# Where side work is issued in a Mamba-2 scan: one step per piece of the scan instead of one behind the projection, and later exponentials in three groups

## The chip, the cores and the metric

The kernel runs on one core of a Trainium2 chip, as one program from input to output. The metric is the time of one execution on the device in microseconds (us). TensorE (PE) multiplies matrices, with its weight loads shown apart (PEld); VectorE (DVE) does elementwise work on tensors; ScalarE (ACT) does activations, casts and copies; GpSimd (POOL) and SyncE (SP) here mostly issue transfers. ACT and POOL issue transfers too. The granted clock is the share of TensorE's full speed that the throttle allowed in a stretch of time.

## The reference

One layer of a trunk over 528 positions (16 meta tokens and 512 tokens) with 1024 channels:

```
u = rmsnorm(h, mix_norm_w)
proj = u @ w_in                       # pool, z, x, B, C, dt, two gates
y_pool = pool_mixer(u_pool, ...) @ w_pool_up
xbc = silu(causal_depthwise_conv(xbc, conv_w, conv_b))     # width 4
y = ssd_chunked(xs, dt, -exp(a_log), B, C) + xs * d_skip   # 8 groups of 4 heads of 64, state 128, chunks of 128
y = rmsnorm per group (y * silu(z)) * norm_w
h = h + (gate_pool * y_pool + gate_ssd * (y @ w_ssd_out)) @ w_o
v = rmsnorm(h, mlp_norm_w)
out = rmsnorm(h + relu(v @ w_ff1)**2 @ w_ff2, final_norm_w)[:, 16:]
```

In one chunk of ssd_chunked, with a_cs the running sum of dt*a:

```
y_diag = (C B^T * exp(a_cs[l] - a_cs[s]) masked) @ (x * dt)
y_off  = (C @ state before the chunk) * exp(a_cs[l])
state  = exp(a_cs[last]) * state + B^T @ (exp(a_cs[last] - a_cs) * x * dt)
```

## The kernel before, in words

**Precision and weights.** All is float32. A product is made of three matmuls of halves: an operand is split into a high part (ACT casts it, L94, `whi`) and a low part (DVE subtracts, L96, `wlo`), and TensorE multiplies high by high, high by low (L196) and low by high (L198). Weights come in blocks of 128 x 1024 from SP's queue into `raw`, three buffers deep, four deep for `whi` and `wlo`.

**Fewer multiplications.** Some products are made with the seven multiplications of Strassen and Winograd on halves. They need sums of weights and sums of u. A set of *weight sums* (`weight_steps`) is formed in DRAM by transfers on POOL's queue alone (L747 and L753): first copies, then transfers that add, in four rounds for a set of kind fx or f1 and two for f2; each round waits for the one before. *Sums of u* (`sums_of_u`) take, for k = 0 to 3, two tiles of u from DRAM (L869, POOL's queue, tiles `ra` and `rb` of one buffer each), combine them on DVE (`combine`, L874 to L877) and split the two results (`form`, L882 on ACT, L883 on DVE, into `t0h`, `t0l`, `t1h`, `t1l`), after which `ra` and `rb` are free for the next k. In the groups of X_PAIRS (4 to 7) the x part of the projection is made that way (`pair`, tiles `rawp`, loaded at L466, split into `whip`, `wlop`); the weight sums of the sets fx feed it.

**The scan.** Behind the norm and the first projections the program goes through eight groups of heads, g = 0 to 7. `ssd(g)` is the scan of group g, cut by its yields into pieces:

- piece 1: the running sums `abc` of group g are loaded (POOL's queue); B and x are transposed on TensorE (`ptb`, `ptm` at L590, `ptx` at L598); DVE makes `xdt` and `xdd`; ACT makes `eb`, the two exponentials of L610 at which y_off is scaled, the differences of decays (L615, L622 with DVE) and their exponentials (`decay`).
- piece 2: C times B (`pcb`), the states `st` (L650) and the masked decays (L653 on DVE, in place in `abc`).
- pieces 3 and 4: for either half of the group's y, TensorE's `po` (L662, from the states) and `py` (L668, from the masked decays), and DVE's L671 to L675 (`yt`).
- then the norm of the group: squares, sums over partitions (`png`), reciprocals (L691, `rs`), and the split into `yh` and `yl`, which ssd's output product reads.

`group_proj(g + 1)` projects the next group meanwhile: B and C, then x (convolution of four taps, L420 and before, then silu, L422, tile `xc`), a gate in groups 1 to 3, then z with its silu (L563 for both halves at once). In group 4 also `out_half` (half of the output product) and in group 7 `out_part` (L848, `psp`) are among the fill. `weave(a, b, n)` sets the order in which the program is written: one piece of the scan, then one step of the first list in `b` that is not at its end (n steps with n = 2), and again. The lists in `b` are used up one after another:

```
fill = [group_proj(g + 1, ...)]          # or out_part; in group 4 out_half ahead of it
fill.append(sums_of_u(SUMS_AT[g], g))    # g = 0: k = 0; g = 1: k = 1; g = 2: k = 2 and 3
fill.append(weight_sums_at())            # SETS_AT[g] times
```

so sums of u come behind all of the projection, and weight sums last. The engines run their queues in order. Where an instruction is to come behind another in its queue though the data does not ask for it, `tc.issue_after` says so: `combine` behind the masked decays (L653) or the squares, `form` behind the first state or the squares, the exponentials `eb` behind the last silu of x of the same group (`x_ready`), which lies in the projection that goes beside the scan of the group before, and the weight sums' transfers behind a one-column copy on POOL (`seen`) of `mark`, which is a tile that the scan wrote last, so that a round does not start ahead of the scan's piece.

Of the kernel before, what the change touches and what calls it, by code (L numbers as in the profile page):

```python
# [11 lines left out]
AF = mybir.ActivationFunctionType  # L12
# [35 lines left out]
SUMS_AT = {0: (0,), 1: (1,), 2: (2, 3)}  # L48
# [2 lines left out]
BC_PAIRS = ()  # L51
PAIRS = [(k, g) for g in range(G) for k in "bx" if g in (BC_PAIRS if k == "b" else X_PAIRS)]

SETS_AT = {0: 1, 1: 1, 2: 1, 3: 1, 4: 2, 5: 1, 6: 1}
SETS_POOL = 2

PLAIN = 4
# [6 lines left out]
def kernel(ctx: ExitStack, tc, xT, x, w, fx, f1, f2, vec, fnw, out):  # L64
# [344 lines left out]


    mark, first_part = [None], [True]
    x_ready, filled = {}, {}

    def conv(dst, src, ct):
        n = dst.shape[-1]
# [92 lines left out]
    def group_proj(g, cur, gate=None):  # L508

        first = g == 0  # L510
        xc, bt, ct, zt = cur

        def plain(dst, t, skip):
            if first and (dst is bt or dst is ct):
                view = viewB if dst is bt else viewC
            else:
                runs, view = wide(psum2(f"px{g}_{t}"), skip)
                proj(runs, block(), X if first else U)
            conv(dst, first_raw(t, view, skip) if first else view, t)

        def z_half(ps, i):

            with tc.issue_after(done[0].ins) if g == 1 else nullcontext():
                wt = block()
            proj(narrow(ps), wt, X if first else U)

        bcs = ((bt, 16 + g, 0), (ct, 24 + g, NM - 4))
        xs = ((xc[:, 0, :], 2 * g, 0), (xc[:, 1, :], 2 * g + 1, 0))
        both = g in BC_PAIRS
        for kind, ts, paired in (("b", bcs, both), ("x", xs, g in X_PAIRS)):  # L530
            if paired:
                r = raw_pair(kind, g)
                yield from pair(kind, g, r)
                for (dst, t, skip), src in zip(ts, r):
                    conv(dst, src[:, skip:], t)
                yield
            else:
                for t in ts:
                    plain(*t)
                    filled.setdefault(g - 1, mm[0])  # L540
                    yield
            if both:
                i = 0 if kind == "b" else 1
                ps = psum2(f"pz{g}_{i}")[:, :SEQ]
                z_half(ps, i)
                act.activation(zt[:, i, :], ps, AF.Silu)
                yield
        if both:
            return
        if gate is not None:  # L550
            gate_pool(gate)
            yield
        ps = psum2(f"pz{g}")
        for i in range(2):
            z_half(ps[:, i * SEQ : (i + 1) * SEQ], i)
        zf = zt.rearrange("p i t -> p (i t)")
        if first:
            dve.tensor_tensor(zt, ps.rearrange("p (i t) -> p i t", i=2),
                              rsb[:, NM:].unsqueeze(1).to_broadcast([P, 2, SEQ]), op=ALU.mult)
            act.activation(zf, zf, AF.Silu)  # L560
            mark[0] = zf[:, :1]
        else:
            act.activation(zf, ps, AF.Silu)  # L563
        yield


# [3 lines left out]
    def ssd(g, cur):  # L570
# [35 lines left out]
        ap = abc.rearrange("p (i j) l -> p i j l", j=2)  # L606
        for j in range(2):
            js = slice(64 * j, 64 * j + 64)
            with tc.issue_after(x_ready[g].ins):
                act.activation(eb[js, :, :], ap[js, :, j, :], AF.Exp)  # L610
        dm = abc.rearrange("p r (c l) -> p r c l", c=4)
        for r in range(R):
# [89 lines left out]

    done, abc_load, masked, y_first, squared, b_meta, x_decayed = {}, {}, {}, {}, {}, {}, {}

    def weave(a, b, n):

        end = object()
        a = [a]
        while a or b:
            for s in [a] + [b] * n:  # L710
                if s and next(s[0], end) is end:
                    s.pop(0)

    m1 = {}

# [22 lines left out]
    def weight_steps():  # L738
        t = sets.pop(0)
        src = {"fx": fx, "f1": f1, "f2": f2}[t[0]][t[1]]  # L740
        o = {n: wsum[(*t, n)] for n in SUMS[t[0]]}
        put = nc.gpsimd.dma_start
        put(o["t1"], src[B11])
        end = put(o["s3"], src[B12])
        if "t2" in o:
            put(o["t2"], src[B22])
            end = put(o["t4"], src[B21])  # L747
        yield end
        put(o["t1"], src[B12], accum_op=ALU.add)
        yield put(o["s3"], src[B22], accum_op=ALU.add)  # L750
        if "t2" in o:
            yield put(o["t2"], o["t1"], accum_op=ALU.add)
            yield put(o["t4"], o["t2"], accum_op=ALU.add)  # L753
# [3 lines left out]
            pass  # L757
        return end

    def weight_sums_at():  # L760
        for _ in range(len(SUMS[sets[0][0]])):
            if not steps:
                steps.append(weight_steps())
            at = pool.tensor_copy(seen, mark[0])
            with tc.issue_after(at.ins):
                next(steps[0])
            yield
        assert next(steps.pop(), None) is None

    steps = []  # L770

    cur = group_tiles(0)
    early = weight_sums_at()
# [87 lines left out]
    def sums_of_u(ks, g):  # L861

        one, two = HF

        def load(k):
            a, b = raw_pair("u", k)
            with tc.issue_after(abc_load[g].ins):
                for t, kk in ((a, k), (b, k + 4)):
                    nc.gpsimd.dma_start(t, u_d[kk])  # L869
            return a, b  # L870

        def combine(a, b, behind):
            with tc.issue_after(behind[g].ins):
                dve.tensor_tensor(b[:, two], a[:, two], b[:, two], op=ALU.subtract)  # L874
                dve.tensor_tensor(a[:, two], a[:, one], a[:, two], op=ALU.subtract)
                dve.tensor_tensor(a[:, one], b[:, two], a[:, one], op=ALU.subtract)
                dve.tensor_tensor(b[:, one], b[:, one], a[:, one], op=ALU.add)  # L877

        def form(k, n, src, behind):
            hi, lo = T[n, "h", k], T[n, "l", k]  # L880
            with tc.issue_after(behind[g].ins):
                act.copy(hi, src)  # L882
            dve.tensor_tensor(lo, src, hi.bitcast(F32), op=ALU.subtract)  # L883

        t = load(ks[0])
        yield
        combine(*t, masked)
        yield
        form(ks[0], "0", t[0], y_first)
        yield  # L890
        form(ks[0], "1", t[1], y_first if len(ks) > 1 else squared)
        if len(ks) > 1:
            t = load(ks[1])
        yield
        if len(ks) > 1:
            yield
            combine(*t, squared)
            form(ks[1], "0", t[0], squared)
            yield
            form(ks[1], "1", t[1], squared)  # L900
            yield

    for g in range(G):
        nxt = group_tiles(g + 1) if g + 1 < G else None
        fill = [group_proj(g + 1, nxt, GATE_AT.get(g))] if nxt else [out_part()]
        if g == 4:
            fill = [out_half()] + fill
        if g in SUMS_AT:
            fill.append(sums_of_u(SUMS_AT[g], g))
        for _ in range(SETS_AT.get(g, 0)):  # L910
            fill.append(weight_sums_at())
        weave(ssd(g, cur), fill, 2 if g == 4 else 1)
        cur = nxt
    gc_stack.close()
    st_stack.close()
# [904 lines left out]
```

## Time and profile before

| | |
|---|---|
| time, median of 3 runs | 1026.56 us (1025.18 to 1030.13) |
| profiled execution | 1029.08 us, span 1027.4 us |
| mean granted clock | 0.992 |
| PE, PEld busy | 1001.4 us (97%), 881.5 us (86%) |
| DVE, ACT, POOL busy | 798.1 (78%), 611.9 (60%), 111.8 us (11%) |
| transfers | 184.51 MB, mean 180 GB/s |
| chain that ended last | PE 80%, DMA 6%, DVE 5%, ACT 5%, issue 3% |
| the scan of groups 0 to 7 | about 71 to 480 us of the span (first ptm to last py, L590 and L668) |

The profile is one execution; its times are microseconds from the start of its span. Busy counts an engine's instructions without the issue of transfers. PE and PEld overlap. A timeline row is start, duration, engine, line, operation, result <- operands, shapes, count, and in brackets the idle time just before it on that engine and what ended it. A row of a stretch is start:end, length, busy time (and instructions) of PE, PEld, DVE, ACT and POOL, the granted clock, the mean busy share of the 16 DMA engines, and GB/s.

### The profile page before, as it was taken

The page shows a single profiled execution, that of the slowest core. Times are in us where ns is not written, and L with a number is a line of the kernel's source. Part 1 is how long each engine was busy: PE and PEld are TensorE (multiplying, and loading weights), DVE is VectorE, ACT ScalarE, POOL GpSimd, SP SyncE. Part 2 cuts the span into 40 slices and gives each one's busy share as a digit, 9 for nine tenths or more (in the row PEclk, how much of TensorE's full clock was granted, in tenths as well). Part 3 has the DMA queues.
Part 4 walks back from the last instruction along what each step waited for, and adds up shares of the span by engine and source line. Part 5 has one row for each costly group of instructions (what it writes and reads, how often), then busy time and mean ns, then how long its engine had stood idle before and what let it go on. Part 6 is the DMA issues. An engine that isn't in the chain of part 4 may idle for free.

```text
span 1027.4 us, 15622 instructions
## 1 busy us (share of the span) xinstructions
PE 1001.4 (97%) x6047; PEld 881.5 (86%) x6047; DVE 798.1 (78%) x1153; ACT 611.9 (60%) x860; POOL 111.8 (11%) x183
## 2 busy tenths in 40 slices
PE   9998999998999979999999999999999999999997
PEld 7888998988888878987988888887889999999986
DVE  7976897967753668888589755876988888888885
ACT  7666859574934475775434433457756665665654
POOL 0420201010202201011330000231000000000000
PEclk9999999998999989999999999999999999999999
DMA  7593866444868937275895642789454554455432
GB/s 255 171 304 109 241 171 174 143 136 139 231 189 248 294 69 233 64 226 148 241 280 143 217 174 80 257 213 314 102 174 149 158 173 153 154 172 157 143 103 82
DMA packets 61291, 184.51 MB, mean 180 GB/s; under 512 B 7073, under 2 KB 8417, under 8 KB 60193
## 3 DMA queue, kind: packets, MB, share of 16 engines
q1 hardware_dynamic: 39456, 109.00, 32.5%
q0 software_dynamic: 18880, 69.67, 26.4%
q10 hardware_dynamic: 2880, 4.84, 1.3%
q8 instruction: 47, 0.77, 0.3%
q14 instruction: 28, 0.22, 0.1%
HBM read 173.13 MB, written 58.59 MB: 226 GB/s over the span
## 4 chain that ended last, share of the span: by engine, by line
PE 80%; DMA 6%; DVE 5%; ACT 5%; issue 3%; POOL 1%; SPq 0%; ACTq 0%; DVEq 0%; POOLq 0%
PE px L1439 8%; PE alpha L1507 6%; PE px L196 6%; PE px L1442 4%; PE px L198 3%; PE alpha L1510 3%; PE pz L196 3%; PE pgs L196 3%; PE pqx L485 2%; PE po L662 2%; DMA rawp<-in_fx 2%; PE py L668 1%; PE pso L128 1%; PE pz L198 1%; PE pso L129 1%
## 5 line engine op out<-in xcount | busy, mean ns | idle before, releaser
L94 ACT CAST whi<-raw 128x1024 fp32r<-128x1024 f32 (+2 forms) x90 | 90.0, 1012 | 87.5 <-DMA raw<-in_w 23.1
L96 DVE TENSOR_TENSOR wlo<-raw,whi 128x1024 fp32r<-128x1024 f32 (+2 forms) x90 | 105.0, 1172 | 40.1 <-ACT whi L94 31.0
L196 PE MATMUL px<-uh,whi 128*128 128x264 f32 (+1 forms) x320 | 83.3, 297 | 0.0
L198 PE MATMUL px<-ul,whi 128*128 128x264 f32 (+1 forms) x320 | 81.1, 290 | 0.0
L1214 DVE TENSOR_TENSOR ht<-ht,alpha 128x1024 f32<-128x1024 f32 x35 | 42.7, 1219 | 29.1 <-PE alpha L1507 29.1
L196 PEld LDWEIGHTS px<-uh,whi 128*128 128x128 f32 x320 | 62.2, 194 | 1.0 <-issue 0.7
L198 PEld LDWEIGHTS px<-ul,whi 128*128 128x128 f32 x320 | 61.9, 194 | 0.5 <-issue 0.2
L1137 ACT CAST shi<-rawf 128x1024 fp32r<-128x1024 f32 x42 | 44.2, 1052 | 28.7 <-PE alpha L1510 18.3
L1507 PE MATMUL alpha<-shi,hh 128*128 128x512 f32 x140 | 55.2, 394 | 0.0
L1510 PE MATMUL alpha<-shi,hl 128*128 128x512 f32 x140 | 54.7, 391 | 0.0
L1138 DVE TENSOR_TENSOR slo<-rawf,shi 128x1024 fp32r<-128x1024 f32 x42 | 51.2, 1219 | 0.6 <-ACT shi L1137 0.6
L1442 PE MATMUL px<-vsl,shi 128*128 128x256 f32 x192 | 47.4, 280 | 0.0
L1439 PE MATMUL px<-vsh,shi 128*128 128x256 f32 x192 | 47.4, 281 | 0.0
L196 PE MATMUL pz<-uh,whi 128*128 128x512 f32 x112 | 43.9, 392 | 1.3 <-ACT yh L698 1.3
L198 PE MATMUL pz<-ul,whi 128*128 128x512 f32 x112 | 43.8, 391 | 0.0
L196 PE MATMUL px<-uh,wlo 128*128 128x264 f32 (+1 forms) x320 | 42.3, 285 | 0.0
L196 PEld LDWEIGHTS px<-uh,wlo 128*128 128x128 f32 x320 | 40.5, 191 | 0.0
L1507 PE MATMUL alpha<-slo,hh 128*128 128x512 f32 x140 | 37.4, 389 | 0.0
L1439 PEld LDWEIGHTS px<-vsh,shi 128*128 128x128 f32 x192 | 36.2, 189 | 0.9
L1442 PEld LDWEIGHTS px<-vsl,shi 128*128 128x128 f32 x192 | 36.1, 188 | 0.9
L1442 PE MATMUL px<-vl,shi 128*128 128x256 f32 x144 | 36.1, 283 | 0.0
L1439 PE MATMUL px<-vh,shi 128*128 128x256 f32 x144 | 36.0, 282 | 0.0
(597 smaller groups left out, 3070.0 us busy)
## 6 DMA issues: line engine op xcount, KB each, us to landing
raw<-in_w SPq DMA_DIRECT2D x96, 512.0 KB, 4.6
f_t<-in_f POOLq DMA_DIRECT2D x38, 512.0 KB, 7.7
f_s<-in_f POOLq DMA_DIRECT2D x26, 512.0 KB, 8.1
b<-in_f SPq DMA_DIRECT2D x21, 512.0 KB, 4.6
rawf<-in_f SPq DMA_DIRECT2D x36, 256.0 KB, 3.0
rawf<-f_t SPq DMA_DIRECT2D x36, 256.0 KB, 2.9
abc<-acs_d POOLq DMA_DIRECT2D x8, 1024.0 KB, 6.0
f_t<-f_t POOLq DMA_DIRECT2D x12, 512.0 KB, 6.8
```

The costliest lines, as they stand in the source:

```text
L94: act.copy(hi[:, c], raw[:, c])
L96: dve.tensor_tensor(lo[:, c], raw[:, c], hi[:, c].bitcast(F32), op=ALU.subtract)
L196: pe.matmul(o, wt, rhs[0][k][:, c], start=part == 0 and k == 0, stop=part == 1 and k == NK - 1)
L198: mm[0] = pe.matmul(o, wt, rhs[1][k][:, c], start=False, stop=False)
L485: pe.matmul(o, wk, f[k][0], start=start and not low and k == 0, stop=stop and low == 1 and k == 3, skip_group_check=True)
L1137: splits.append((act.copy(hi, src), dve.tensor_tensor(lo, src, hi.bitcast(F32), op=ALU.subtract)))
L1138: dve.tensor_tensor(lo, src, hi.bitcast(F32), op=ALU.subtract)))
L1214: added[0] = dve.tensor_tensor(o, o, src, op=op)
L1439: pe.matmul(ps, m, f[k][0], start=start and not low and k == 0, stop=stop and low == 1 and k == 3, skip_group_check=True)
L1442: pe.matmul(ps, m, f[k][1], start=False, stop=False, skip_group_check=True)
L1507: pe.matmul(ps[t], hh[:, p, seg, st], m, start=bool(first and not low and p == 0), stop=bool(last and low and p == 1), skip_group_check=True)
L1510: pe.matmul(ps[t], hl[:, p, seg, st], m, start=False, stop=False, skip_group_check=True)
```

## The change

It has two parts.

*Order of the sums.* `weave` gets a fourth argument, `side`, a list of generators of which each takes one step in every round, behind the piece of the scan and the step of the fill. `sums_of_u` and `weight_sums_at` go into `side` instead of behind the projection in `fill`. `weight_sums_at(n)` runs n whole sets in a row with steps of its own, and ends with one more copy of `mark` for each set. The yields of `sums_of_u` are set anew: with two ks the second form of the first k and the load of the next one come in the same step, and the second form of the last k comes one step later. `SETS_AT` gives group 1 two sets and group 4 one (before, one and two).

*Exponentials.* `z_ready[g]` holds z's last silu of group g's projection. In groups 5 to 7 the two exponentials `eb` are issued behind it, and no longer behind `x_ready[g]`, the last silu of x.

```diff
--- before.py
+++ after.py
@@ -51,7 +51,7 @@
 BC_PAIRS = ()
 PAIRS = [(k, g) for g in range(G) for k in "bx" if g in (BC_PAIRS if k == "b" else X_PAIRS)]
 
-SETS_AT = {0: 1, 1: 1, 2: 1, 3: 1, 4: 2, 5: 1, 6: 1}
+SETS_AT = {0: 1, 1: 2, 2: 1, 3: 1, 4: 1, 5: 1, 6: 1}
 SETS_POOL = 2
 
 PLAIN = 4
@@ -409,7 +409,7 @@
 
 
     mark, first_part = [None], [True]
-    x_ready, filled = {}, {}
+    x_ready, z_ready, filled = {}, {}, {}
 
     def conv(dst, src, ct):
         n = dst.shape[-1]
@@ -543,7 +543,7 @@
                 i = 0 if kind == "b" else 1
                 ps = psum2(f"pz{g}_{i}")[:, :SEQ]
                 z_half(ps, i)
-                act.activation(zt[:, i, :], ps, AF.Silu)
+                z_ready[g] = act.activation(zt[:, i, :], ps, AF.Silu)
                 yield
         if both:
             return
@@ -557,10 +557,10 @@
         if first:
             dve.tensor_tensor(zt, ps.rearrange("p (i t) -> p i t", i=2),
                               rsb[:, NM:].unsqueeze(1).to_broadcast([P, 2, SEQ]), op=ALU.mult)
-            act.activation(zf, zf, AF.Silu)
+            z_ready[g] = act.activation(zf, zf, AF.Silu)
             mark[0] = zf[:, :1]
         else:
-            act.activation(zf, ps, AF.Silu)
+            z_ready[g] = act.activation(zf, ps, AF.Silu)
         yield
 
 
@@ -606,7 +606,7 @@
         ap = abc.rearrange("p (i j) l -> p i j l", j=2)
         for j in range(2):
             js = slice(64 * j, 64 * j + 64)
-            with tc.issue_after(x_ready[g].ins):
+            with tc.issue_after((z_ready if g in X_PAIRS[1:] else x_ready)[g].ins):
                 act.activation(eb[js, :, :], ap[js, :, j, :], AF.Exp)
         dm = abc.rearrange("p r (c l) -> p r c l", c=4)
         for r in range(R):
@@ -702,14 +702,15 @@
 
     done, abc_load, masked, y_first, squared, b_meta, x_decayed = {}, {}, {}, {}, {}, {}, {}
 
-    def weave(a, b, n):
+    def weave(a, b, n, side):
 
         end = object()
         a = [a]
-        while a or b:
+        while a or b or side:
             for s in [a] + [b] * n:
                 if s and next(s[0], end) is end:
                     s.pop(0)
+            side = [s for s in side if next(s, end) is not end]
 
     m1 = {}
 
@@ -757,17 +758,15 @@
             pass
         return end
 
-    def weight_sums_at():
-        for _ in range(len(SUMS[sets[0][0]])):
-            if not steps:
-                steps.append(weight_steps())
-            at = pool.tensor_copy(seen, mark[0])
-            with tc.issue_after(at.ins):
-                next(steps[0])
-            yield
-        assert next(steps.pop(), None) is None
-
-    steps = []
+    def weight_sums_at(n=1):
+        for _ in range(n):
+            steps = weight_steps()
+            while True:
+                at = pool.tensor_copy(seen, mark[0])
+                with tc.issue_after(at.ins):
+                    if next(steps, None) is None:
+                        break
+                yield
 
     cur = group_tiles(0)
     early = weight_sums_at()
@@ -887,29 +886,27 @@
         combine(*t, masked)
         yield
         form(ks[0], "0", t[0], y_first)
-        yield
-        form(ks[0], "1", t[1], y_first if len(ks) > 1 else squared)
         if len(ks) > 1:
+            form(ks[0], "1", t[1], y_first)
             t = load(ks[1])
         yield
+        yield
         if len(ks) > 1:
-            yield
             combine(*t, squared)
             form(ks[1], "0", t[0], squared)
             yield
-            form(ks[1], "1", t[1], squared)
-            yield
+        form(ks[-1], "1", t[1], squared)
+        yield
 
     for g in range(G):
         nxt = group_tiles(g + 1) if g + 1 < G else None
         fill = [group_proj(g + 1, nxt, GATE_AT.get(g))] if nxt else [out_part()]
         if g == 4:
             fill = [out_half()] + fill
+        side = [weight_sums_at(SETS_AT.get(g, 0))]
         if g in SUMS_AT:
-            fill.append(sums_of_u(SUMS_AT[g], g))
-        for _ in range(SETS_AT.get(g, 0)):
-            fill.append(weight_sums_at())
-        weave(ssd(g, cur), fill, 2 if g == 4 else 1)
+            side.append(sums_of_u(SUMS_AT[g], g))
+        weave(ssd(g, cur), fill, 2 if g == 4 else 1, side)
         cur = nxt
     gc_stack.close()
     st_stack.close()
```

## The prediction

> **What bounds the kernel now.** I read the page's engine table first, then who waited for whom, then the busy times by stretch, and last the timelines around the stretches in which TensorE stood still.
>
> ```profile
> PE 1001.4 (97%) x6047; PEld 881.5 (86%) x6047; DVE 798.1 (78%) x1153; ACT 611.9 (60%) x860; POOL 111.8 (11%) x183
> PE ptm L590 <- ACT xc L422: 5.7, 1, 5.7
> PE po L662 <- DVE st L650: 3.5, 3, 1.7
> 225.00:250.00 25.00, 20.84 (x147) 18.59 (x146) 19.80 (x36) 15.44 (x25) 0.56 (x1) 0.86 0.18 54
> 235.00:240.00 5.00, 2.38 (x21) 1.75 (x19) 5.00 (x9) 3.25 (x5) 0.00 (x0) 0.86 0.00 0
> 240.00:245.00 5.00, 5.00 (x23) 4.51 (x22) 2.50 (x5) 0.64 (x2) 0.00 (x0) 0.50 0.70 210
> 360.00:375.00 15.00, 9.34 (x52) 8.97 (x51) 8.44 (x17) 12.54 (x19) 0.81 (x1) 0.78 0.51 107
> 370.00:375.00 5.00, 5.00 (x25) 5.00 (x24) 3.42 (x8) 4.95 (x12) 0.00 (x0) 0.50 0.00 0
> ```
>
> The first line is the engines' busy time: TensorE is busy for 1001.4 of the span's 1027.4 us, so 26.0 us is all the idle time there is, and work taken from another engine is worth only what it takes out of that, or out of a lowered clock. The next two are the longest waits of TensorE. The rest are stretches: start and end, length, busy time of PE, PEld, DVE, ACT, POOL, then the granted clock, DMA share and GB/s. Two stretches of the scan hold most of what can be won there. At the start of group 3's scan TensorE is idle for 25.00 - 20.84 = 4.16 us, and over 240 to 245 it runs at 0.50. At the start of group 5's it is idle for 15.00 - 9.34 = 5.66 us and then runs at 0.50 over 370 to 375. Half a clock for 5 us is 2.5 us of work lost; with 0.86 of the 2.38 busy us before it, 0.3 more. So group 3's stop costs 4.16 + 2.5 + 0.3 = 7.0 us and group 5's 5.66 + 2.5 = 8.2 us: 15.2 together.
>
> The clock is where a rule speaks against my sum. In 225 to 250 no single wait is over 1.7 us (second row of waits), and the clock fell to 0.50 all the same. The Trainium skill, TensorE: Matmul & The Clock Gate, Part 1, says that the clock is halved after an idle window of about 3.4 us. By that, group 3's short waits would cost no clock and only 4.16 us could be won there, 2.8 us less; this trace has the halved clock after short waits, and the sum goes by the trace.
>
> **Why they stop: group 3.**
>
> ```profile
> 205.34 0.57 POOL L869 DMA_DIRECT2D rau<-u_d  x1 [1.73 <-DVE t0l L883]
> 208.00 0.86 POOL L869 DMA_DIRECT2D rbu<-u_d  x1
> 215.96 0.43 DVE L874 TENSOR_TENSOR rbu<-rau,rbu 128x264 f32<-128x264 f32 x1 [8.49 <-DMA rbu<-u_d]
> 217.72 3.38 DVE L691 RECIPROCAL rs<-rs 128x128 f32<-128x128 f32 x4
> 232.60 2.29 DVE L653 TENSOR_TENSOR abc<-abc,cbm 128x2048 f32<-128x2048 f32 x1 [1.49 <-ACT abc L622]
> DMA to landing us min/median/max: 3.4/8.0/11.6
> ```
>
> These are timelines (start, length, engine, line) and the landing times of the transfers of u_d. The fourth k of the sums of u is loaded at 205 to 208, because its two tiles have one buffer each and the third k was read out of them only then. DVE reached its combination (L874) with nothing landed and stood 8.49 us with everything of group 3 queued behind: the reciprocals of rs2, and through them ACT's decays, and L653, at which TensorE's py waits.
>
> **The change there.** In the changed program sums_of_u is a side list that takes one step per piece of the scan, no longer one after the whole of group_proj. On DVE the four instructions of k=2 now stand between the state updates of group 2 and its y, so that both tiles are free earlier.
>
> ```profile
> 186.53 0.41 DVE L650 TENSOR_TENSOR st<-st,pst 128x256 f32<-128x256 f32 x1
> 188.58 0.69 DVE L671 TENSOR_TENSOR yt<-po,eb 128x512 f32<-128x512 f32 x1 [0.97 <-PE po L662]
> 198.61 0.68 DVE L675 TENSOR_TENSOR yt<-yt,zt 128x512 f32<-128x512 f32 x1
> 199.21 0.42 DVE L875 TENSOR_TENSOR rau<-rau 128x264 f32<-128x264 f32 x1
> 204.34 0.70 DVE L883 TENSOR_TENSOR t0l<-rau,t0h 128x528 fp32r<-128x528 f32 x1
> ```
>
> The last readers (t0l, t1l, L883, 0.70 each) come just behind the first y product (188.58 + 0.69 = 189.3), so rau is free at about 190 and rbu at 191.3, 15 to 16 us before the 205.34 and 208.00 of now. With the median landing of 8.0 us rbu is there at 199.3. DVE's order has its combination behind the second half of y, which now ends at 199.3 (L675 at 198.6), and the two weight splits that moved out (2.4 us) about pay for the four combining steps and two L883 that moved in (1.7 + 1.4). So the wait of 8.49 becomes 0 to 2 us, and at the maximum landing of 11.6, 4 us. What is late next: raw blocks are prefetched three deep, and the split of the block before (wlo29) now stands behind that combination, so the cast of block 32 slips to about 208 on ACT, with xc3's silu, gp5, rs2 and the decays behind it. Counted on from there by the rows of now the decays end at about 226 to 228 instead of 232.57, and TensorE, without its gaps, comes to the py of group 3 at 233.5, after L653's 2.29 and the state updates. I take 6.5 of the 7.0 us as won; bounds 3 (landing at the maximum) and 7.0.
>
> ```profile
> 71.13 0.56 POOL L869 DMA_DIRECT2D rau<-u_d  x1 [4.88 <-PE pgp L196]
> 94.90 0.41 DVE L650 TENSOR_TENSOR st<-st,pst 128x256 f32<-128x256 f32 x1
> 85.00:95.00 10.00, 6.77 (x50) 6.16 (x49) 7.97 (x13) 7.42 (x10) 0.00 (x0) 0.84 0.00 1
> ```
>
> The other three combinations also move forward on DVE. For k=0 the loads go out behind the first four copies of set fx1, which wait for xdt0, at about 78.5 instead of 71.1; DVE comes to it after the last state update of group 0, near 95.3, so there are 16 us for them, and over 85 to 95 the DMA engines are idle. For k=1 and k=2 the loads have 10 us and more. Cost 0, and the cover is that margin.
>
> **Group 5.**
>
> ```profile
> 343.88 0.82 POOL L747 DMA_DIRECT2D f_t<-in_f  x1
> 365.25 0.81 POOL L753 DMA_DIRECT2D f_t<-f_t  x1 [8.28 <-DMA f_t<-f_t]
> 355.00:360.00 5.00, 5.00 (x24) 4.14 (x23) 1.90 (x2) 0.31 (x2) 0.81 (x1) 1.00 1.07 304
> 348.43 1.02 SPq L466 DMA_DIRECT2D rawp<-in_fx  x2
> 353.42 0.80 SPq L466 DMA_DIRECT2D rawp<-fx_t  x2
> DMA to landing us min/median/max: 2.5/4.6/11.5
> 360.43 1.05 ACT L94 CAST whip<-rawp 128x1024 fp32r<-128x1024 f32 x1 [5.12 <-DMA rawp<-in_fx]
> 364.13 0.64 ACT L422 ACTIVATE xc<-xc 128x528 f32<-128x528 f32 x1 [1.92 <-DVE xc L420]
> 364.79 1.28 ACT L610 ACT_TABLE_LOAD   x1
> 366.09 1.06 ACT L610 ACTIVATE eb<-abc 64x1024 f32<-64x1024 f32 x1
> 367.16 1.28 ACT L422 ACT_TABLE_LOAD   x1
> 368.45 0.64 ACT L422 ACTIVATE xc<-xc 128x528 f32<-128x528 f32 x1
> 369.15 0.69 PE L590 MATMUL ptm<-ident,xc 128*128 128x128 f32 x2 [5.66 <-ACT xc L422]
> ```
>
> Here two things stand in a row. Two sets of weight sums (SETS_AT 4: 2) run on POOL's queue from 320 to 373 behind group 4's out_half, the DMA share is 1.07, and the first pair of group 6's weights, issued at 348.43, lands so late that ACT stands 5.12 us at its cast (the longest landing of rawp is 11.5, the median 4.6). Then, between the two silus of xc5, ACT takes a table for exp, the first exponential eb and a table back: 1.28 + 1.06 + 1.28 = 3.62 us, while ptm waits for the second silu.
>
> The change takes both away. Set f12 is spread over group 4's own pieces (its copies behind xdt4, its sums behind st3_4 and yt4), one set moves to group 1, and the stretch 325 to 360 keeps only weight loads. With 4.6 us the pair of 348.43 lands at 353.0 and the next one, issued at 353.42, at 358.0. The exponentials come behind z's silu. On the other side the cast of that next pair (1.05) now stands between the two silus. Counted by the rows: the cast of 360.43 moves up by its wait of 5.12 to about 355.3, DVE's steps of xc5 end near 360.0 instead of 365.6, the first silu stands near 359, the cast behind it, and the second silu ends at 360.8. TensorE comes to ptm, now directly behind pz5, at 360.9. A stop of 0 to 1.5 us is left; I take 7.2 of the 8.2 us as won, bounds 0 (both pairs land as late as now: 353.42 + 11.5 + 1.05 + 0.64 = 366.6, which is 5.7 us of idle TensorE and the half clock again) and 8.2.
>
> **Groups 6 and 7 pay a little.**
>
> ```profile
> 422.96 1.04 ACT L622 ACTIVATE abc<-abc 128x1024 f32<-128x1024 f32 x1
> 424.04 2.29 DVE L653 TENSOR_TENSOR abc<-abc,cbm 128x2048 f32<-128x2048 f32 x1 [0.62 <-ACT abc L622]
> 427.66 1.09 PE L668 MATMUL py<-abc,xdt 128*64 128x128 f32 x14
> 465.81 0.74 PE L848 MATMUL psp<-yh,whi 128*128 128x512 f32 x2 [0.68 <-ACT whi L816]
> ```
>
> There was no stop at ptm to win in them. Both exponentials and one cast now come behind rs5, so the decays of group 6 end about 1.2 us later than 424.0. DVE's order puts L653 behind two of bt7's steps and a state update, so it ends near 429.5 instead of 426.3. TensorE now does one po and four matmuls of the next projection before py, which it then reaches near 428.2: 1.2 us of waiting, bounds 0 and 2. In group 7 the cast at which psp already waits 0.68 slips by the later exponential: 0.8 us, bounds 0 and 1.5. Eight table loads fewer on ACT (52 to 44) are 8 x 1.28 = 10.3 us of an engine that is 60% busy; they count only where named above. The thirteen extra one-column copies on POOL are hidden, since POOL is 11% busy. TensorE has the same matmuls, and behind the scan the order is the same on all engines.
>
> **Sum.** -6.5 - 7.2 + 1.2 + 0.8 = -11.7 us on the profiled execution, from 1029.1 to 1017.4. That run lies 2.5 us above the median of the three timed ones, 1026.56, and from the median it is 1014.9: I say 1015. Half a per cent is 5.1 us, about what a measurement of this kernel can tell from no change.
>
> ```profile
> 120.00:140.00 20.00, 19.89 (x163) 18.89 (x162) 18.27 (x27) 15.41 (x21) 2.35 (x4) 1.00 0.86 182
> ```
>
> **Rivals.** (1) *One stop stays.* The sums are not fewer, they only move, and a pair or rbu that lands at its maximum brings one of the two back: 11.7 - 7.2 or 11.7 - 6.5 leaves 4.5 to 5.2 us, 1021.4 to 1022. For it: the 11.5 and 11.6 above. Against it: DMA share 0.00 over 235 to 240, into which f11's copies move. The Trainium skill, DMA: Bandwidth & Descriptors, section Issuing engines are not separate DMA queues, says that transfers issued from all engines run on the same 16 DMA engines and interleave; by that, moved sums slow what they meet at the new place as they did at the old. Chance 0.16, on the edge of half a per cent, so half counts as faster. (2) *Nothing to measure.* The waits are replaced: block 32's late cast holds ACT's chain of group 3, and the cast between the silus holds group 5. Each gives back over half: -3 - 3.5 + 2 = -4.5 or less, 1022 to 1027. Chance 0.12. (3) *Slower.* DVE, 18.27 us busy of the 20 above in group 1, now has the combinations in front of its own y and state updates, and their loads stand in POOL's queue behind weight sums that wait for one another. If the loads of k=0, 1 and 2 each come as late as k=3's did (8.49 us of DVE, 7.0 of TensorE), that is +21.0 - 11.7 = +9.3, 1036. It decides from the point where rbu lands more than some 2 us after DVE's last state update; for k=0 that is 97, against an issue at 79 and a longest landing of 11.6, so the trace is mostly against it. Chance 0.10. The forecast keeps 0.62.
>
> **Numbers.** The forecast's own range is 1011 (nothing left at either stop, -15.2 + 0.5) to 1019. The low end is taken to 1008, since 2.4 us more of short waits in groups 5 and 7 may go, and the high end to 1025, which holds (1) and most of (2). Faster by over 0.5%: 0.62 + 0.08 = 0.70; within it: 0.08 + 0.12 = 0.20; slower 0.10.
>
> **What would show it.** Right: DVE's idle time before L874 under 3 us in all four; no wait of TensorE at ptm over 2 us; the clock at 1.00 through groups 3 and 5; eight table loads fewer; a new wait of about 1 us at py in group 6. Wrong: TensorE waiting for wlo, png or po in groups 0 to 2, or a cast of rawp with several us of DMA wait in front of it.

## The result and the profile after

The changed kernel takes 1023.74 us, the median of 20 runs (1017.79 to 1030.06); the kernel before, in 20 runs beside it, 1027.67 (1021.65 to 1030.13). The ratio is 0.9955 with a 95% interval of 0.994 to 0.997, that is 4.6 us of gain, 3.1 to 6.2 by the interval. The forecast was 11.7. The profiled execution took 1026.01 us with a span of 1024.3, and the engine table and the waits of TensorE read:

```profile
PE 1000.8 (98%) x6047; PEld 879.5 (86%) x6047; DVE 798.1 (78%) x1153; ACT 603.1 (59%) x852; POOL 116.5 (11%) x192
PE po L662 <- DVE st L650: 4.1, 3, 2.0
PE png L686 <- ACT qhg L310: 3.3, 1, 3.3
PE psp L847 <- ACT whi L815: 1.2, 1, 1.2
```

The 5.7 us at ptm are gone, and with eight table loads fewer ACT is busy for 8.8 us less. But po waits for st no less than before (4.1 us, then 3.5), and png has a wait of 3.3 us that was not there. To see where each stage gained, take the start of L591 (xddm, DVE's first step of a group) in either timeline, up to the square root of group 7's norm (ACT, L689). The first and last rows that bound groups 1 to 3, before and then after:

```profile
119.72 0.42 DVE L591 TENSOR_TENSOR xddm<-ptm,wmeta 128x256 f32<-128x256 f32 x1 [1.34 <-PE ptm L590]
273.49 0.42 DVE L591 TENSOR_TENSOR xddm<-ptm,wmeta 128x256 f32<-128x256 f32 x1 [0.36 <-PE ptm L590]
```

```profile
120.14 0.42 DVE L591 TENSOR_TENSOR xddm<-ptm,wmeta 128x256 f32<-128x256 f32 x1 [1.55 <-PE ptm L590]
277.78 0.41 DVE L591 TENSOR_TENSOR xddm<-ptm,wmeta 128x256 f32<-128x256 f32 x1
```

| us | group 1 | 2 | 3 | 4 | 5 | 6 | 7 | 1 to 3 | 4 to 7 |
|---|---|---|---|---|---|---|---|---|---|
| before | 49.7 | 54.1 | 50.0 | 96.4 | 43.5 | 43.2 | 32.3 | 153.8 | 215.4 |
| after | 54.8 | 52.6 | 50.3 | 88.9 | 41.9 | 42.6 | 33.5 | 157.6 | 206.9 |

Groups 4 to 7 won 8.5 us, where the prediction had 5.2 for groups 5 to 7. Groups 1 to 3, which were to win 6.5, lost 3.9. L591 is a step of DVE and can itself come late: before, the one of group 3 stood in DVE's queue behind the 8.49 us, so group 2 looks long (54.1) though TensorE is never idle in it. TensorE's own idle time between these instants is 0.11 us in group 1 before and 3.34 after, 4.16 and then 3.19 in group 3, and 8.96 and then 3.36 in groups 4 to 7 together; its mean clock is 1.00 and then 0.94 in group 1, 0.93 and then 0.97 in group 3. So group 3's stop is smaller but not gone, and group 1 has a new one. The stretches of the changed kernel that answer to those shown of before, and group 1's new stop (columns as in the prediction):

```profile
225.00:250.00 25.00, 21.81 (x168) 20.45 (x166) 20.65 (x37) 18.32 (x28) 4.16 (x8) 0.93 0.53 152
240.00:245.00 5.00, 3.02 (x21) 2.27 (x20) 5.00 (x9) 2.59 (x3) 0.18 (x1) 0.71 0.39 111
360.00:375.00 15.00, 15.00 (x100) 13.64 (x99) 10.85 (x21) 11.96 (x20) 1.25 (x3) 1.00 0.57 174
155.00:160.00 5.00, 2.89 (x13) 2.06 (x11) 2.28 (x5) 3.46 (x4) 0.53 (x1) 1.00 0.89 364
160.00:165.00 5.00, 3.78 (x9) 3.02 (x10) 2.79 (x3) 4.81 (x7) 1.92 (x4) 0.52 0.79 158
```

Group 5 runs through at full clock. Group 3 still stands for 3.19 us. Group 1 now stands for 2.11 + 1.22 = 3.33 us and then runs at 0.52. The timelines of ACT, and of POOL's and TensorE's side of it, say why:

```profile
141.78 0.83 POOL L750 DMA_DIRECT2D f_t<-in_f  x1
149.09 0.53 POOL L744 DMA_DIRECT2D f_t<-in_f  x1
149.61 0.52 POOL L745 DMA_DIRECT2D f_s<-in_f  x1
156.48 1.05 ACT L94 CAST whi<-raw 128x1024 fp32r<-128x1024 f32 x1 [4.57 <-DMA raw<-in_w]
157.44 1.05 ACT L680 ACTIVATE sqg<-yt 128x1024 f32<-128x1024 f32 x1
160.57 0.60 ACT L310 CAST qhg<-sqg 128x512 fp32r<-128x512 f32 x1
161.22 0.80 PE L686 MATMUL png<-qhg,ones_r 128*128 128x512 f32 x1 [3.33 <-ACT qhg L310]
204.38 0.42 DVE L873 TENSOR_TENSOR rbu<-rau,rbu 128x264 f32<-128x264 f32 x1
203.21 1.05 ACT L94 CAST whi<-raw 128x1024 fp32r<-128x1024 f32 x1 [4.48 <-DMA raw<-in_w]
212.22 1.05 ACT L94 CAST whi<-raw 128x1024 fp32r<-128x1024 f32 x1 [4.97 <-DMA raw<-in_w]
235.42 2.29 DVE L653 TENSOR_TENSOR abc<-abc,cbm 128x2048 f32<-128x2048 f32 x1 [1.50 <-ACT abc L622]
242.25 0.80 PE L662 MATMUL po<-ct,st 128*128 128x128 f32 x2 [1.98 <-DVE st L650]
```

In group 1, the adds of the first set of weight sums go out at 142 and the first copies of the second set at 149, behind the first half of y. The block of weights that is loaded beside them comes late, and ACT stands 4.57 us at its cast, with the square of group 1's y, and so png, behind that cast. In group 2 the fourth combination of u (L873, L874 before) no longer waits at all. But ACT now stands 4.48 and 4.97 us at casts of raw, and with it the same chain as before: the silu of xc3, rs2, the decays, L653. (The first of these two waits has another cause, shown below with the sums of u alone.) The landing times of raw over 135 to 175 us, before and then after:

```profile
DMA to landing us min/median/max: 3.5/4.3/5.0
```

```profile
DMA to landing us min/median/max: 3.5/6.8/8.1
```

### The profile page after: what moved, and what is told of

Read it like the earlier page. It is cut to its first block, busy times and chain, and to the rows that moved or that the text cites. A ratio compares the mean times of both kernels' runs of the same rounds, so it can differ in the third digit from the quotient of the medians.

```text
span 1024.3 us, 15645 instructions
## 1 busy us (share of the span) xinstructions
PE 1000.8 (98%) x6047; PEld 879.5 (86%) x6047; DVE 798.1 (78%) x1153; ACT 603.1 (59%) x852; POOL 116.5 (11%) x192
## 4 chain that ended last, share of the span: by engine, by line
PE 77%; DMA 8%; ACT 6%; DVE 5%; issue 3%; POOL 1%; SPq 0%; ACTq 0%; DVEq 0%; POOLq 0%
PE px L1436 8%; PE alpha L1504 6%; PE px L196 6%; PE px L1439 4%; DMA raw<-in_w 4%; PE pz L196 4%; PE alpha L1507 3%; PE px L198 3%; PE pgs L196 3%; PE pqx L485 2%; PE pz L198 2%; PE py L668 2%; PE pf L129 1%; PE pf L128 1%; PE wo_alpha L1198 1%
## 5 line engine op out<-in xcount | busy, mean ns | idle before, releaser
L94 ACT CAST whi<-raw 128x1024 fp32r<-128x1024 f32 (+2 forms) x90 | 90.2, 1011 | 96.8 <-DMA raw<-in_w 32.5
L1439 PE MATMUL px<-vsl,shi 128*128 128x256 f32 x192 | 47.4, 280 | 0.0
L1436 PE MATMUL px<-vsh,shi 128*128 128x256 f32 x192 | 47.4, 281 | 0.0
```

The source lines that it names most:

```text
L94: act.copy(hi[:, c], raw[:, c])
L1436: pe.matmul(ps, m, f[k][0], start=start and not low and k == 0, stop=stop and low == 1 and k == 3, skip_group_check=True)
L1439: pe.matmul(ps, m, f[k][1], start=False, stop=False, skip_group_check=True)
```

## The experiments

Theory A: what costs is the bytes of the weight sums that now move beside the loads of raw in groups 1 and 2, above all the set moved into group 1 and the set of four rounds that it pushes into group 2. Theory B: the interleaving costs, by the order on the queues or by ACT's and DVE's own work, whatever the transfers. Each expectation says what A and B mean for its run. All ratios below are to the kernel before, in five rounds each; 0.1% is 1.03 us. The stage columns come from one profile each.

| kernel | ratio (95%) | groups 1 to 3 | groups 4 to 7 |
|---|---|---|---|
| before | 1 | 153.8 | 215.4 |
| changed | 0.9955 (0.994 to 0.997) | 157.6 | 206.9 |
| changed, SETS_AT as before | 0.9922 (0.9899 to 0.9946) | 149.1 | 206.9 |
| changed, exponentials as before | 1.0020 (0.9999 to 1.0042) | 152.8 | 216.9 |
| changed, few columns in groups 1, 2 | 1.0080 (1.0049 to 1.0112) | 147.5 | 208.0 |
| changed, weight sums last in groups 1, 2 | 0.9908 (0.9876 to 0.9939) | 148.4 | 206.9 |
| before + sums of u at the side | 0.9941 (0.9923 to 0.9959) | 145.4 | 213.4 |
| before + SETS_AT | 0.9900 (0.9875 to 0.9925) | 149.4 | 207.5 |
| before + weight sums at the side | 1.0012 (0.9992 to 1.0033) | 153.0 | 212.5 |
| before + exponentials | 0.9998 (0.9977 to 1.0019) | 153.4 | 214.0 |
| before + sums of u + SETS_AT | 0.9884 (0.9856 to 0.9913) | 146.9 | 207.0 |
| the same + exponentials | 0.9876 (0.9845 to 0.9907) | 148.0 | 206.8 |
| the same, second set in group 6, not 1 | 0.9898 (0.9872 to 0.9924) | 145.5 | 208.1 |

How far one profile can be trusted: the second and the fourth kernel have the same code in groups 0 to 3 and differ by 157.6 - 152.8 = 4.8 us there; the first and "before + exponentials" have it too, and differ by 0.4. Group 0 (44.0 and 47.4 us in the two kernels with the sums of u alone at the side, without and with SETS_AT) and what follows the scan (538.5 to 543.0, the kernel that defers columns left aside) also differ between kernels whose code is the same there. So totals are compared by the timed runs.

**The set put back.**

```diff
-SETS_AT = {0: 1, 1: 2, 2: 1, 3: 1, 4: 1, 5: 1, 6: 1}
+SETS_AT = {0: 1, 1: 1, 2: 1, 3: 1, 4: 2, 5: 1, 6: 1}
```

> The changed kernel with SETS_AT as before: one set of weight sums in group 1 and two in group 4, all else as changed. Measured from L591 (xddm) of a group to L591 of the next: before 49.65 us for group 1 and 50.0 for group 3, changed 54.8 and 50.3. Theory A (the second set in group 1, and the four-round set that it pushes into group 2, hold up the loads of raw blocks there): group 1 back to about 49.7, group 3 to about 45, no cast of raw waiting over 3 us in groups 1 and 2, the median some 8 to 10 us under the changed one, about 1014 to 1016, if group 5 keeps its gain; 7 us of it go if group 4's two sets bring group 5's stop back. Theory B (rounds spread over the pieces of the scan meet the loads of raw whichever set it is): groups 1 and 3 stay at about 54 and 50, the median within 2 us of the changed kernel or above it.

3.4 us under the changed kernel (plus or minus 2.9). Group 1 takes 50.8 and 2 takes 48.5, while group 3 stays at 49.9: A's sign, with half its size, and A's 45 for group 3 is missed. Group 5 keeps its gain though group 4 has two sets again, so spreading them is enough to free the pair of 348. Group 1 is not back where it was, though its second set is gone. With one set spread, the cast before the square of y still waits 3.42 us, and png 2.04:

```profile
157.18 1.05 ACT L94 CAST whi<-raw 128x1024 fp32r<-128x1024 f32 x1 [3.42 <-DMA raw<-in_w]
161.76 0.50 PE L686 MATMUL png<-qhg,ones_r 128*128 128x512 f32 x1 [2.04 <-ACT qhg L310]
```

The clock stays at 1.00 behind that wait. The second set makes the cast wait 4.57 us and png 3.33, and there the clock falls.

**The exponentials put back.**

```diff
-            with tc.issue_after((z_ready if g in X_PAIRS[1:] else x_ready)[g].ins):
+            with tc.issue_after(x_ready[g].ins):
```

> The changed kernel with the exponentials of groups 5 to 7 behind x's silu again. If the table loads between the two silus of xc5 are a part of the stop at ptm: 2 to 3.6 us of waiting at ptm of group 5 come back, some 3 to 5 us with the clock, median 1026 to 1029, and L591 of group 4 to group 5 grows from 88.9 by as much. If all of the gain of group 5 came from the weights that land earlier: group 4 to 5 within 1 us of 88.9, the median within 2 us of the changed kernel. Groups 1 to 3 as in the changed kernel in either case.

6.7 us over the changed kernel (plus or minus 2.7), more than expected, and not where it was expected: group 4 to 5 is 90.6, only 1.7 more, but group 5 takes 45.8 and group 6 takes 46.2 (41.9 and 42.6 in the changed kernel). Its timelines at the end of group 5:

```profile
397.00 1.05 ACT L94 CAST whi<-raw 128x1024 fp32r<-128x1024 f32 x1 [3.38 <-DMA raw<-in_w]
399.15 1.05 ACT L94 CAST whi<-raw 128x1024 fp32r<-128x1024 f32 x1 [1.10 <-DMA raw<-in_w]
405.59 1.28 ACT L610 ACT_TABLE_LOAD   x1
406.89 1.06 ACT L610 ACTIVATE eb<-abc 64x1024 f32<-64x1024 f32 x1
407.96 1.28 ACT L422 ACT_TABLE_LOAD   x1
409.95 0.69 PE L590 MATMUL ptm<-ident,xc 128*128 128x128 f32 x2 [4.66 <-ACT xc L422]
```

Late blocks put xc6's silus late, and the 3.62 us of tables and exponential come on top.

**Sums of u alone at the side.**

`weave` and the yields of `sums_of_u` are as in the changed kernel. Besides:

```diff
...
+        side = []
         if g in SUMS_AT:
-            fill.append(sums_of_u(SUMS_AT[g], g))
+            side.append(sums_of_u(SUMS_AT[g], g))
         for _ in range(SETS_AT.get(g, 0)):
             fill.append(weight_sums_at())
-        weave(ssd(g, cur), fill, 2 if g == 4 else 1)
+        weave(ssd(g, cur), fill, 2 if g == 4 else 1, side)
...
```

> The kernel before with the sums of u alone as a side list, in the changed order of steps; weight sums still last in the fill, exponentials and SETS_AT as before. Theory A: DVE no longer stands 8.5 us at the combination of k=3, raw blocks land as before, group 3's stop is mostly gone: L591 of group 3 to group 4 falls from 50.0 to about 45, group 1 stays at 49.7, group 5 keeps its stop; median 5 to 7 us under the kernel before, about 1021. Theory B (what holds group 3 is ACT's and DVE's own work in groups 2 and 3, whatever lands): group 3 stays within 1.5 us of 50.

0.9941, 6.1 us of gain: what the prediction gave to group 3's stop (6.5). It shows as 5.5 in group 2 and 2.1 in group 3, not as 5 in group 3, because the L591 between them had stood behind the 8.49 us. Its stretch from 220 to 245 us has TensorE busy throughout:

```profile
220.00:245.00 25.00, 25.00 (x203) 23.32 (x203) 21.31 (x33) 14.05 (x19) 0.58 (x1) 1.00 0.34 107
```

So ACT's and DVE's own work does not hold group 3, as B and the prediction's second rival had it. The casts that were late in the changed kernel read here:

```profile
151.93 1.05 ACT L94 CAST whi<-raw 128x1024 fp32r<-128x1024 f32 x1 [1.21 <-DMA raw<-in_w]
189.77 1.22 DVE L96 TENSOR_TENSOR wlo<-raw,whi 128x1024 fp32r<-128x1024 f32 x1
191.07 0.33 SPq L86 DMA_DIRECT2D raw<-in_w  x1
195.44 1.05 ACT L94 CAST whi<-raw 128x1024 fp32r<-128x1024 f32 x1 [3.84 <-DMA raw<-in_w]
202.01 1.06 ACT L94 CAST whi<-raw 128x1024 fp32r<-128x1024 f32 x1 [1.88 <-DMA raw<-in_w]
```

The wait of 3.84 us in group 2 (4.48 in the changed kernel) thus comes from the order on DVE: the split `wlo` that frees a buffer of raw stands behind the combination and the forms of u, so the load is issued only at 191.07. That is the prediction's own point about wlo29, and here it costs TensorE nothing. The next block takes 5.2 us from its issue at 196.81 to its cast; in the changed kernel, with the weight sums spread beside it, 8.3 (203.94 to 212.22). The order on DVE also uses up the margin in group 1: without the sums of u at the side no cast there waits for raw in the profiles of the kernel before, of SETS_AT alone and of the weight sums alone; with them two casts wait 1.10 and 1.21 us, and a slower landing comes on top.

**SETS_AT alone.** The edit is the reverse of the first, in the kernel before.

> The kernel before with only SETS_AT changed: two sets in group 1, one in group 4, all behind the projection as before. If the second set in group 1 is what costs, wherever its rounds are put: 2 to 5 us are lost in groups 1 and 2, and group 5 wins 4 to 6 of its 8, as the pair of 348 lands early and the table loads stay; median 1024 to 1028. If it costs only in the spread order: groups 1 to 3 as before, the median 1021 to 1024.

0.9900, 10.3 us, better than either theory expected. Group 1 is untouched (49.7) with two sets behind its projection, and groups 4 and 5 win 5.9 and 2.5. Groups 1 to 3 take 4.3 us less than before, which is within what two profiles of the same code differ by there (4.8). The table loads are still between the silus of xc5, and ptm does not wait:

```profile
355.05 0.65 ACT L422 ACTIVATE xc<-xc 128x528 f32<-128x528 f32 x1 [2.54 <-DVE xc L420]
355.71 1.28 ACT L610 ACT_TABLE_LOAD   x1
358.08 1.28 ACT L422 ACT_TABLE_LOAD   x1
359.38 0.64 ACT L422 ACTIVATE xc<-xc 128x528 f32<-128x528 f32 x1
360.08 0.44 PE L590 MATMUL ptm<-ident,xc 128*128 128x128 f32 x2
```

**Weight sums alone at the side.** `weight_sums_at` as changed, sums of u last in the fill.

```diff
...
+        side = [weight_sums_at(SETS_AT.get(g, 0))]
         if g in SUMS_AT:
             fill.append(sums_of_u(SUMS_AT[g], g))
-        for _ in range(SETS_AT.get(g, 0)):
-            fill.append(weight_sums_at())
...
```

> The kernel before with the weight sums alone as a side list (rounds spread over the pieces of the scan); sums of u last in the fill, SETS_AT and exponentials as before. Theory A (spreading is what costs: a round that is released at a piece of the scan runs beside the loads of raw for the next projection): the casts of L94 wait 29 us or more for raw in total (23.1 before, 32.5 changed, 25.7 and 18.2 in the two kernels of the last round that don't spread), group 1 takes 1 to 3 us longer than 49.7, group 6 2 to 3 us longer than 43.2, and what group 5 wins by the earlier pair does not outweigh it: median 1026 to 1033. Theory B (spreading itself costs nothing, only the set moved into group 1 does): groups 1, 2 and 6 within 1 us of before, group 5 wins 5 us or more, median 1019 to 1023.

1.0012, not told apart from no change. The casts of L94 wait 30.7 us for raw (23.1 before), as A expected. By the one profile group 4 wins 6.0 by the earlier pair, while group 3 (+3.9) and group 6 (+2.9) lose; group 1 does not (49.5), where A expected it: with the sums of u last, no cast there waits for raw.

**Exponentials alone.**

> The kernel before with the exponentials of groups 5 to 7 behind z's silu, nothing else. If the table loads between the silus are a part of their own of group 5's stop: L591 of group 4 to 5 falls from 96.4 by 2 to 3.6 us, groups 6 and 7 lose up to 1 us each, median 1024 to 1026. If the late pair alone sets it: within 1 us of 96.4 and the median within 1.5 us of before, or up to 2 us above it by groups 6 and 7.

0.9998: nothing in the total, as the second reading had it, while the stage moves as the first did: group 4 to 5 falls by 3.1 us. Group 5, which neither named, and group 7 take 1.2 more each.

**Sums of u and SETS_AT, weight sums last; and with the exponentials.**

> Sums of u as a side list, and SETS_AT as changed, but the weight sums last in the fill as before and the exponentials as before. Theory A: the two gains add, group 3's stop by u (6.3 us by the median, groups 2 and 3 together 7.5 in the trace) and group 5's by the sets (10.2): median 1011 to 1014, L591 of group 2 to 4 near 97, of group 4 to 6 near 132. Theory B (two sets in group 1 collide with the sums of u of group 2, as in the changed kernel): groups 2 and 3 stay near 103, median 1017 to 1019.

> As the third of these (sums of u as a side list, SETS_AT as changed, weight sums last in the fill), and the exponentials of groups 5 to 7 behind z's silu. Against that third kernel: if the exponentials help only where the spread rounds hold up the silus, the same within 1.5 us or 1 to 2 us slower by groups 6 and 7; if they take a stop of their own away in group 5 (1.7 us between the changed kernel and that with the exponentials put back), 1 to 3 us faster, median 1009 to 1012.

0.9884 and 0.9876, medians 1015.85 and 1014.89, against 1026.88 for the kernel before beside them. The first median lies between A's range and B's. The two gains add in part: 11.9 us where 6.1 and 10.3 would be 16.4; the stages (97.9 for groups 2 and 3, 131.6 for 4 and 5) are those of A. The exponentials add 0.8 us, plus or minus 4.3: not settled.

**The same rounds with few columns.** In groups 1 and 2 each transfer of the weight sums moves 64 of 1024 columns; the rest is summed in group 7.

```diff
+        c = slice(64, 1024) if t else slice(0, 64 if thin else 1024)
...
+        put = lambda o, i, **kw: nc.gpsimd.dma_start(o[:, c], i[:, c], **kw)
...
+        side = ([weight_sums_at(len(deferred), late=deferred)] if g == 7
+                else [weight_sums_at(SETS_AT.get(g, 0), g in (1, 2))])
```

> The changed kernel with the same rounds of weight sums at the same places in groups 1 and 2, but each transfer there moves 64 of the 1024 columns only; the other 960 columns of these three sets are summed in group 7. Theory A (what costs in groups 1 to 3 is the bytes of these transfers beside the loads of raw): in group 1 the median landing of raw falls from 6.8 to about 4, ACT's casts wait under 2 us each, L591 of group 1 to group 4 falls from 157.7 to 146 to 150 (145.4 with the sums of u alone as a side list). Groups 7 and after may lose several us to the deferred sums, so the stages decide, not the total. Theory B (the order on POOL's queue and on DVE costs, whatever the bytes): group 1 to 4 stays at 155 or more.

Groups 1 to 3 take 147.5 us, with every round, copy and queue position as in the changed kernel. Landing of raw over 135 to 175 us, its worst casts in groups 1 and 2, and the stretch in which png had stood:

```profile
DMA to landing us min/median/max: 3.7/3.8/4.4
146.06 1.05 ACT L94 CAST whi<-raw 128x1024 fp32r<-128x1024 f32 x1 [1.27 <-DMA raw<-in_w]
197.22 1.05 ACT L94 CAST whi<-raw 128x1024 fp32r<-128x1024 f32 x1 [3.94 <-DMA raw<-in_w]
155.00:160.00 5.00, 5.00 (x24) 4.12 (x23) 5.00 (x7) 4.97 (x7) 3.27 (x4) 1.00 0.68 148
```

The bytes are the cause in group 1, and B falls there: both profiles with the full bytes have late raw blocks (median landing 6.8 and, with the exponentials put back, 7.1 us) and a wait at png (3.3 and 2.7), and take 157.6 and 152.8. In group 2 two casts still wait 3.94 and 2.34 us, over the 2 that A allowed; the first is the one that waits 3.84 with the sums of u alone. The 1.0080 of the whole comes with the deferred columns: what follows the scan takes 561.3 us.

**Weight sums last in groups 1 and 2 only.**

```diff
-        side = [weight_sums_at(SETS_AT.get(g, 0))]
+        side = []
+        (fill if g in (1, 2) else side).append(weight_sums_at(SETS_AT.get(g, 0)))
```

> The changed kernel, with the weight sums of groups 1 and 2 alone put last in the fill again. Theory A: groups 1 to 3 as where no group spreads them (148.0 from L591 of group 1 to group 4, against 157.7), groups 4 to 7 as in the changed kernel (206.8): median 8 us under it, 1014 to 1016. Theory B (spreading costs in groups 0, 3 and later too): the median stays above 1018.

0.9908: 4.8 us under the changed kernel (plus or minus 3.6), with 148.4 and 206.9 in the stages as A expected. The median, 1018.64, is above A's 1014 to 1016 and just above B's bound of 1018; the stages speak for A, the total for little more than half of its size.

**The second set in group 6.**

> Sums of u as a side list, exponentials of groups 5 to 7 behind z's silu, weight sums last in the fill, and SETS_AT with one set in each of groups 0 to 5 and two in group 6. Theory A (a set costs where its rounds meet a stage that waits for weights): groups 1 to 3 as with the sums of u alone (145.4), groups 4 to 6 as with one set in group 4 (206.8 to the end of the scan, if group 7 bears the second set): median 1011 to 1014, 1 to 3 us under the kernel with two sets in group 1. Rival (group 7's weights for out_part then come late as group 5's did): group 6 and 7 longer by 4 us or more, median 1016 or more.

0.9898, median 1017.57, over A's range. Groups 1 to 3 are as fast as with the sums of u alone (145.5), groups 4 to 7 take 1.3 more than with two sets in group 1. The median is one that the rival named, but its sign is missing: groups 6 and 7 take 42.5 and 33.5 us, as without the second set. The total is not told apart from the kernel with two sets in group 1.

## Why the prediction was right and wrong

**Right: group 5.** 7.2 us were forecast, and group 4 to 5 gave 7.5, with 1.6 more behind it: 9.1 together in one profile each, over the 8.2 that the prediction had as the most. The first cause named, the pair issued at 348 under two sets, is right: SETS_AT alone brings it, and so does spreading the sets. The second, the table loads between the silus, had no price of its own here: with the pair early the second silu still ends in time, and the exponentials alone change the time by -0.2 us, plus or minus 2.2. They pay only where late blocks push the silus, as they do with the weight sums spread (6.7 us).

**Right: sums of u.** The wait of 8.49 us at the fourth combination goes, and by itself this is worth 6.1 us, forecast 6.5. In the changed kernel itself group 3 keeps 3.19 us of its 4.16 idle. Groups 6 and 7 were to pay 1.2 and 0.8. Group 6 won 0.6: the wait at py did not come, and TensorE stands 0.05 us there in place of 0.73. Group 7 took 1.2 more up to its square root, but TensorE's idle time in it grew by 0.35 only (1.18 to 1.53).

**Wrong: the new place of the weight sums.** This is the step that failed. The prediction said of group 5 that "one set moves to group 1" and priced only what leaves group 4, not what arrives. The four rounds there (two sets of two), the four-round set in group 2 in place of one of two rounds, and the spreading of both beside the loads of raw were costed at nothing. One set's copies did go into the idle DMA time around 235 us that the prediction pointed to, but the rounds of group 2's set went to where raw blocks, u and the next abc load: the DMA share over 200 to 220 us rose.

```profile
200.00:220.00 20.00, 20.00 (x104) 17.02 (x103) 11.30 (x18) 12.44 (x16) 5.55 (x8) 1.00 0.72 202
```

```profile
200.00:220.00 20.00, 20.00 (x111) 17.51 (x111) 14.58 (x21) 10.20 (x12) 3.77 (x5) 1.00 0.95 285
```

The rows are before and after. Moving the set does no harm by itself (10.3 us faster with SETS_AT alone), nor do the sums of u at the side (6.1 faster). It is the spreading that costs, and in group 1, by the profiles, only where the sums of u have used up the margin of the raw blocks. The term's size: 8.1 us between the changed kernel and the one that differs only in putting the weight sums last everywhere (plus or minus 3.5), and 4.8 of them (plus or minus 3.6) in groups 1 and 2. The missing gain is 11.7 - 4.6 = 7.1. The first rival had the mechanism in its sentence that moved sums slow what they meet at the new place, and the second named ACT's chain of group 3, but as alternatives to the forecast with 0.16 and 0.12. The third named group 1, but by DVE's work and the loads of u. The sign that the prediction gave for being wrong did appear: TensorE waits for png in group 1. The Trainium skill, DMA: Bandwidth & Descriptors, section Issuing engines are not separate DMA queues, says that transfers of all queues share the same engines and interleave. The 4.3, 6.8 and 3.8 us of raw's landing agree. A price has to come from such landings at the new place, and the prediction took none for raw.

**The clock.** Three kernels have the one wait at png in group 1: 3.33 us of it go with a clock of 0.52 over 160 to 165 us, 2.74 with the exponentials put back with 0.66, and 2.04 with the sets put back with 1.00. The Trainium skill, TensorE: Matmul & The Clock Gate, Part 1, puts the lowering after an idle window of some 3.4 us. The 3.33 and the 2.04 agree with that, the 2.74 only roughly. In group 3, waits of 1.20 and 1.98 us with 0.49 us of work between them go with 0.71 over the 5 us that hold the second, which that rule alone doesn't give.

**Open.** Of the 8.1 us, 4.8 lie in groups 1 and 2; where the rest lies is not shown, since the intervals are as wide as the rest. That the bytes slow the raw blocks is shown by stages and landings of single profiles, not by a total, as the kernel with few columns pays for its deferred sums. How far the loss in groups 1 to 3 varies between executions is known from two profiles only (157.6 and 152.8).

## What to carry to other kernels

Price a moved transfer twice: by what it stops delaying, and by what is loading at the place where it arrives, with that place's own landing times and the casts that wait for them. Work that is released by the pieces of a stage runs beside that stage's own loads, so spreading it evened out POOL's queue here and not the demand on the transfers. Two parts can share one margin: in group 1 neither part made TensorE wait alone, but the sums of u took the slack of the raw blocks, and the spread weight sums then had none. Where a change has several parts, look which of them win the same stop: here the earlier pair was to be had by SETS_AT or by spreading, and the better kernel (0.9876 against 0.9955) takes the first and leaves the weight sums last.

## What was not expected of the hardware

Copies and adds of 512 KB between places in DRAM, issued from POOL, raised the median landing of a 512 KB weight block over 135 to 175 us from 4.3 to 6.8 us and its maximum from 5.0 to 8.1 (7.1 and 9.1 in a second profile of the same code there); with a sixteenth of the bytes and the same number of transfers it was 3.8 and 4.4. Runs of one kernel lie within about 12 us of each other (1017.79 to 1030.06).
